# Twelve channel blocks of a hybrid gMLP and attention step by seven block products over the token halves, with the latent projection ahead of them

## The chip, the cores and the metric

The kernel runs on one core of a Trainium2 chip. The metric is the device time of one execution in microseconds (us), as the median of several runs.

Engines are called as the profile calls them: PE (matrix products and transposes), DVE, ACT and POOL (elementwise work), SP (issues most of the DMAs here).

## What is computed

1152 tokens (1024 samples, 128 prompt) of width 1024 go through one projection `w_in`, whose columns feed two head groups; both end in one output projection.

```python
h = _rmsnorm(x, norm_g) * (1 + scale) + shift
u, v, g_a, c_q, c_kv, k_rope, g_b = _split_in(h @ w_in)
a_out = _chunk_mlp(u, v, w_s, b_s, g_v) * jax.nn.silu(g_a)      # gelu(u) * mixed, gated
q = (_rmsnorm(c_q, q_norm_g) @ w_uq).reshape(B, L, MLA_HEADS, QK_NOPE + QK_ROPE)
ckv = _rmsnorm(c_kv, kv_norm_g)
...
y = jnp.concatenate([a_out, attn * jax.nn.silu(g_b)], axis=-1) @ w_o
return x + gate * y
```

`u`, `g_a` and `g_b` have 512 channels each: 12 blocks of 128, numbered 0 to 11 in the kernel (0 to 3 are `u`, 4 to 7 `g_a`, 8 to 11 `g_b`). `v` has 512 columns; `c_q`, `c_kv` and `k_rope` together have 448 (here: the latents, `z`). All is in float32, which the kernel feeds to PE as a high and a low half (type fp32r): each product is three matmuls, high by high, high by low, low by high.

## The kernel before

Tokens are cut into nine tiles of 128 (tile 8 is the prompt), and the 1024 inputs into NK = 8 chunks `k`. The modulated input `h` stands transposed in three tiles `area0` to `area2`, each of 384 tokens, high and low for every `k`. By the time of the profiled execution the stages are:

- 0 to 58 us, prologue: x and the adaLN weights `ada` arrive by DMA, PE makes the modulation (L331, strips of 32 rows by 256) and the transposes, ACT and DVE split `h`, PE begins the `v` projection (L360 to L362) of tiles 0 to 4.
- 58 to 139 us: a list scheduler (`class Plan`) orders steps that were given an engine, a cost, needs, a priority and counted resources. In it stand `v` of the other tiles, the position mixing, and the first channel blocks (L632, 384 columns).
- 139 to 253 us: blocks 3 to 11 by the loop `for i in range(3, 12)`, each for three groups of 384 tokens (`channels`, `passes3`, L151 to L153). The weights of a block come as one load `w2r` (512 KB) and are split into `w2h` (POOL, L108) and `w2l` (DVE, L105, through `lo_of`). ACT applies GELU or SiLU, POOL multiplies the result into `mixA` (L693, L640 in the planned part). Beside it the adaLN gate sums are made on DVE: `matvec` multiplies and adds eight 256-wide rows (L310, L312) for two conditions, four times; PE sums them over the partitions (`gate_row`, L716). The latent weights `w_q` are loaded and split here too (L108, L301 on POOL).
- 253 to 318 us: the latents `z` of nine tiles (`z_chunk`, L940 to L942, 448 columns), with their statistics, the transposes of `c_q`, the query weights (`fold`) and most queries (`q_nope`, `q_rope`) beside them, in an order made by `merged` and `later`.
- 318 to about 332 us, transition: keys and the last queries; then scores, softmax and attention until 535 us, and the output projection until the end. Both are ordered by lists of steps.

The order within each engine is the program's order (the four compute engines are scheduled by hand); SP issues the DMAs in program order.

Of the kernel before, what the change touches and what calls it, by code (L numbers as in the profile page):

```python
# [18 lines left out]
P = 128  # L19
NT = 9  # L20
# [8 lines left out]
W1 = 8  # L29
W2 = 0  # L30
# [10 lines left out]
class Plan:  # L41
# [8 lines left out]
    def run(self):  # L50
# [3 lines left out]
        while left:  # L54
# [4 lines left out]
            for s in left:  # L59
                _, _, key, eng, cost, fn, deps, takes, gives, lag = s  # L60
                if self.free[eng] > now + 1e-6 or any(self.made.get(d, 1e9) > now + 1e-6 for d in deps):
                    continue
                if any(self.resources[r] < 1 for r in takes):
                    continue
                for r in takes:
                    self.resources[r] -= 1
                fn()
                self.free[eng] = now + cost
                self.made[key] = now + cost + lag
                back += [(now + cost + lag, r) for r in gives]  # L70
                left.remove(s)
                self.log.append((now, cost, eng, key))
                moved = True
                break
            if not moved:
                later = [t for t in (*self.free.values(), *self.made.values(), *(b[0] for b in back)) if t > now + 1e-6]
                assert later, [s[2] for s in left]
# [10 lines left out]
def tile_hymba_step(ctx: ExitStack, tc: tile.TileContext, I, O):  # L88
# [177 lines left out]
    def slot(i, name, shape, dt=F32):  # L266
        return (va if i < 8 else vb).tile([P] + shape, dt, tag=f"S{i}", name=name)
# [3 lines left out]
    area = [ht.tile([P, 16, GW], F32R, tag=f"area{g}", name=f"area{g}") for g in range(3)]  # L271
    hh = {(k, g): area[g][:, 2 * k, :] for k in range(NK) for g in range(3)}
    hl = {(k, g): area[g][:, 2 * k + 1, :] for k in range(NK) for g in range(3)}
# [4 lines left out]
    def load_wv(k):  # L278
        wvr[k] = w1.tile([P, 512], F32, tag="wr", name=f"wvr{k}", bufs=2)
        nc.sync.dma_start(wvr[k], I["w_v"][k])  # L280

    def load_x(t, i):
        xt[t] = slot(i, f"x{t}", [1024])
# [30 lines left out]
    def load_ada(k, slots):  # L314
        out = []
        for hf_ in range(2):
            ch = slot(slots[hf_], f"ada{k}{hf_}", [4, 256])
            nc.sync.dma_start(ch, I["ada_ss"][k][:, hf_ * 4 : hf_ * 4 + 4, :])
            out += [ch[:, i, :] for i in range(4)]
        return out  # L320
# [12 lines left out]
    def mod_copy(k):  # L333
        rowsb[k] = va.tile([P, 256], F32, tag="acc", name=f"rows{k}", bufs=2)
# [14 lines left out]
    def modulate(k, g, c0, c1, ps, cond):  # L349
        w = c1 - c0  # L350
        hf = va.tile([P, GW], F32, tag="hf", name=f"hf{k}{g}{c0}", bufs=3)
        S.activation(hh[k, g][:, c0:c1], ps, AF.Identity, bias=at[:, k, cond, 0:1], scale=at[:, k, cond, 1:2])
        S.activation(hf[:, :w], ps, AF.Identity, bias=at[:, k, cond, 0:1], scale=at[:, k, cond, 1:2])
        lo_of(hl[k, g][:, c0:c1], hf[:, :w], hh[k, g][:, c0:c1])

    def v_terms(k, t, acc):
        g, j = t // 3, t % 3
        sl = slice(j * P, (j + 1) * P)
        a, b = hh[k, g][:, sl], hl[k, g][:, sl]
# [6 lines left out]
    ADA = ((0, 1), (2, 3), (4, 5))  # L366

    def load_k(k):
        if k < NK:
            ada[k] = load_ada(k, ADA[k % 3])  # L370
            load_wv(k)

    wsT = vb.tile([P, 4, P], F32, tag="wsT", name="wsT")
    bsb = vb.tile([P, 4, P], F32, tag="bsb", name="bsb")
    kvg = mc.tile([P, P], F32, tag="kvg", name="kvg")

    w2raw, w2hi, w2lo = {}, {}, {}

    def load_w2(i):
        w2raw[i] = slot(4 + i % 2, f"w2r{i}", [8, P])  # L380
        nc.sync.dma_start(w2raw[i], I["w_t"][i])

    def split_w2(i):
        a, b = ((0, 1), (2, 3), (6, 7))[i % 3]
        w2hi[i] = slot(a, f"w2h{i}", [8, P], F32R)
        w2lo[i] = slot(b, f"w2l{i}", [8, P], F32R)
        pool_copy(w2hi[i], w2raw[i])
        lo_of(w2lo[i], w2raw[i], w2hi[i])
# [27 lines left out]
    def h_pe(k, g):  # L416
        xps[k, g] = pst.tile([P, 512], F32, tag="t", name=f"xT{k}{g}")
        transposes(k, [3 * g, 3 * g + 1, 3 * g + 2], xps[k, g])

    def h_ev(k, g):  # L420
        modulate(k, g, 0, GW, xps[k, g][:, :GW], 0)
# [6 lines left out]
    with tc.manual_schedule(engines=engines):  # L428
# [13 lines left out]
        for t in (0, 1, 2):  # L442
            load_x(t, 6 + t)
        load_k(0)
        for t in (3, 4, 5):
            load_x(t, 6 + t)
# [9 lines left out]
        h_pe(0, 0)  # L456
        ssq1 = vb.tile([P, 3], F32, tag="ssq", name="ssq3", bufs=2)
        square(V, 3, ssq1[:, 0:1])
        h_ev(0, 0)
# [8 lines left out]
        h_pe(0, 1)  # L468
        h_ev(0, 1)
        modulation(1)  # L470
        for k in range(1, NK):
# [23 lines left out]
            if k == 4:  # L495
                load_w2(0)
                load_w2(1)
                nc.sync.dma_start(wsT, I["wsT"])
                nc.sync.dma_start(bsb, I["b_s"].broadcast_to([P, 512]))
                nc.sync.dma_start(kvg, I["kv_g"].broadcast_to([P, P]))  # L500
# [10 lines left out]
    gv, ssv = {}, {}  # L511
    plan = Plan()
    step = plan.add

# [3 lines left out]
    def rsqrt_steps(key, pool, ssq, n, width, tag, prio, deps, before=None):  # L518
        cell = {}

        def begin():
            if before is not None:
                before()
# [5 lines left out]
        step(f"{key}.-1", "V", 0.08, begin, deps, prio)  # L529
        for i in range(count):  # L530
            step(f"{key}.{i}" if i < count - 1 else key, "V", 0.08, lambda i=i: cell["ops"][i](), [f"{key}.{i - 1}"], prio, lag=0.13)
        return cell

    def split_steps(i, deps):
        def hi():
            a, b = ((0, 1), (2, 3), (6, 7))[i % 3]
            w2hi[i] = slot(a, f"w2h{i}", [8, P], F32R)
            w2lo[i] = slot(b, f"w2l{i}", [8, P], F32R)
            pool_copy(w2hi[i], w2raw[i])

        step(f"w2h{i}", "G", 1.01, hi, [f"w2r{i}", *deps], 2)
# [1027 lines left out]
```

## Time and profile before

| | |
|---|---|
| runs | 632.67, 633.30 and 637.25 us, median 633.3 us |
| profiled execution, first to last instruction | 634.2 us, mean granted PE clock 0.987 |
| PE, DVE, ACT, POOL busy | 615.5, 366.3, 257.8 and 182.6 us |
| DMA | 46.3 MB, mean 73 GB/s over the span |

A row of the groups of instructions reads: line, engine, operation, output<-inputs by the program's names, shape and number; then busy time in us and mean ns of one; then the idle time of the engine before them and what ended it. A row of a timeline begins with its start and its duration in us; what stands in brackets is the engine's idle time before it and the instruction that ended it. Durations of pipelined PE instructions overlap, so PE's price is read from the distance of starts or from the chain that ended last. A row of stretches gives for each engine the busy us and the number of instructions, then PE's granted clock, the share of the DMA engines and GB/s.

### The profile page before, as it was taken

The numbers are of one execution on the slowest core, as the hardware profiler recorded it, in microseconds if no ns is written. First come the engines' busy times: TensorE is split into PE (matmuls) and PEld (weight loads), VectorE is DVE, ScalarE is ACT, GpSimd is POOL, SyncE is SP. The second block draws the span as 40 slices with busy tenths as digits, with TensorE's granted clock in tenths as the row PEclk, the third lists the DMA queues.
The fourth block names the chain that finished last, engine by engine and source line by source line (L and its number), as shares of the span: only waits on it lengthen the run. The fifth ranks groups of instructions, "written<-read, shape, count | busy, mean of one in ns | idle before, by whom it ended". The sixth has DMA issues, their size and how long they took to land.

```text
span 634.2 us, 9897 instructions
## 1 busy us (share of the span) xinstructions
PE 615.5 (97%) x3715; PEld 557.2 (88%) x3715; DVE 366.3 (58%) x922; ACT 257.8 (41%) x613; POOL 182.6 (29%) x219
## 2 busy tenths in 40 slices
PE   7799999999999999999989999999999999999995
PEld 6577889999999999999978899999999988888884
DVE  4437447237866200567886665776766755387655
ACT  4355784012111111455456555555555543132212
POOL 2534202344436510233353221332222341000001
PEclk9799999999999999999989999999999999999998
DMA  8976100015023330000010000001000112523311
GB/s 318 321 247 215 66 1 2 1 38 209 18 99 114 125 119 0 26 13 2 0 41 1 1 1 1 1 1 35 34 1 33 34 68 75 192 99 133 105 62 66
DMA packets 17119, 46.32 MB, mean 73 GB/s; under 512 B 1952, under 2 KB 6448, under 8 KB 17072
## 3 DMA queue, kind: packets, MB, share of 16 engines
q1 hardware_dynamic: 16928, 45.51, 20.6%
q8 instruction: 29, 0.48, 0.3%
q10 hardware_dynamic: 144, 0.20, 0.1%
q14 instruction: 18, 0.15, 0.1%
HBM read 40.87 MB, written 4.83 MB: 72 GB/s over the span
## 4 chain that ended last, share of the span: by engine, by line
PE 90%; DVE 3%; DMA 2%; ACT 2%; issue 1%; SPq 1%; POOL 0%; ACTq 0%
PE tp L152 6%; PE tp L632 6%; PE tp L153 6%; PE tp L151 6%; PE pT L1095 5%; PE w L1342 5%; PE w L1343 5%; PE w L1344 5%; PE o L1121 3%; PE o L1119 3%; PE s L1048 3%; PE s L1049 3%; PE o L1120 3%; PE s L1051 3%; PE s L1052 3%; PE s L1050 3%
## 5 line engine op out<-in xcount | busy, mean ns | idle before, releaser
L105 DVE TENSOR_TENSOR pl<-pT,ph 128x512 fp32r<-128x512 f32 x81 | 55.5, 687 | 47.7 <-ACT ph L1099 47.5
L1039 POOL TENSOR_SCALAR e<-e,rs 128x1280 f32<-128x1280 f32 x32 | 42.8, 1337 | 132.3 <-DVE rs L1038 118.0
L153 PE MATMUL tp<-area,w2l 128*128 128x384 f32 x216 | 72.7, 336 | 0.0
L152 PE MATMUL tp<-area,w2h 128*128 128x384 f32 x216 | 72.6, 336 | 0.0
L151 PE MATMUL tp<-area,w2h 128*128 128x384 f32 x216 | 72.6, 336 | 0.0
L1033 ACT ACTIVATE e<-s,nb,scl 128x256 f32<-128x256 f32 x64 | 56.1, 881 | 36.9 <-DVE nb L1027 36.8
L1099 ACT CAST ph<-pT 128x512 fp32r<-128x512 f32 x80 | 45.4, 589 | 42.7 <-PE pT L1095 40.0
L1095 PE MATMUL pT<-ident,e 128*128 128x128 f32 x320 | 47.9, 273 | 0.7 <-DVE pl L105 0.7
L1119 PE MATMUL o<-ph,vh 128*128 128x256 f32 x160 | 47.4, 296 | 0.0
L1121 PE MATMUL o<-ph,vl 128*128 128x256 f32 x160 | 44.7, 280 | 0.0
L105 DVE TENSOR_TENSOR w2l<-w2r,w2h 128x1024 fp32r<-128x1024 f32 x12 | 20.3, 1688 | 42.1 <-POOL w2h L108 42.1
L1120 PE MATMUL o<-pl,vh 128*128 128x256 f32 x160 | 44.6, 279 | 0.0
L1344 PE MATMUL w<-area,ml 128*128 128x512 f32 (+1 forms) x114 | 43.2, 379 | 0.0
L1095 PEld LDWEIGHTS pT<-ident,e 128*128 128x128 f32 x320 | 37.5, 140 | 4.4 <-DVE pl L105 1.5
L151 PEld LDWEIGHTS tp<-area,w2h 128*128 128x128 f32 x216 | 40.7, 188 | 0.6
L152 PEld LDWEIGHTS tp<-area,w2h 128*128 128x128 f32 x216 | 40.7, 188 | 0.2
L153 PEld LDWEIGHTS tp<-area,w2l 128*128 128x128 f32 x216 | 40.7, 188 | 0.0
L1023 DVE TENSOR_REDUCE m<-s 128x1 f32<-128x1024 f32 x32 | 38.9, 1216 | 1.5 <-PE s L1052 1.5
L1048 PE MATMUL s<-kch,area 128*128 128x512 f32 (+2 forms) x100 | 39.1, 391 | 0.0
L632 PE MATMUL tp<-area,w2h 128*128 128x384 f32 x144 | 37.1, 339 | 0.0
L1049 PE MATMUL s<-kcl,area 128*128 128x512 f32 (+2 forms) x100 | 35.5, 355 | 0.0
L1051 PE MATMUL s<-krh,area 128*128 128x512 f32 (+2 forms) x100 | 35.3, 353 | 0.0
(295 smaller groups left out, 1599.7 us busy)
## 6 DMA issues: line engine op xcount, KB each, us to landing
ada<-in_ada_ss SPq DMA_DIRECT2D x16, 512.0 KB, 9.6
w2r<-in_w_t SPq DMA_DIRECT2D x12, 512.0 KB, 3.6
xr<-in_x SPq DMA_DIRECT2D x9, 512.0 KB, 4.6
adag<-in_ada_g SPq DMA_DIRECT2D x8, 512.0 KB
wor<-in_w_o SPq DMA_DIRECT2D x8, 512.0 KB, 3.3
out_y<-y SPq DMA_DIRECT2D x8, 512.0 KB, 3.7
x<-in_x SPq DMA_DIRECT2D x6, 512.0 KB, 9.1
wvr<-in_w_v SPq DMA_DIRECT2D x8, 256.0 KB, 8.4
```

The source lines that it names most:

```text
L105: V.tensor_tensor(lo, src, f32(hi), op=ALU.subtract)
L151: T.matmul(ps, wh, xh, start=j == 0, stop=False)
L152: T.matmul(ps, wh, xl, start=False, stop=False)
L153: T.matmul(ps, wl, xh, start=False, stop=j == n - 1)
L632: T.matmul(tps[i, g][:, :GW], w_[i][:, k, :], x_[k, g], start=k == 0 and j == 0, stop=k == NK - 1 and j == 2)
L1033: S.activation(e[:, sl], src, AF.Exp, bias=nb, scale=scl[:, t : t + 1], accum_out=su[:, i : i + 1])
L1048: T.matmul(ps, qh_, kch[:, sl], start=True, stop=False)
L1095: T.transpose(ps[:, w : w + P], es[t, h][:, c * P : (c + 1) * P], ident)
L1119: T.matmul(o, vh[:, kt, :], ph[:, sl], start=c == 0, stop=False)
L1120: T.matmul(o, vh[:, kt, :], pl[:, sl], start=False, stop=False)
L1121: T.matmul(o, vl[:, kt, :], ph[:, sl], start=False, stop=c == n - 1)
L1344: T.matmul(ps, b, woh[k][:, c0:c1], start=False, stop=k == NK - 1)
```

## The change

**Token projection.** The 1024 sample tokens are cut into two halves `x`, the 1024 inputs into two halves `y`, and `h` lies in four tiles `areas[x, y]` of 512 tokens by 512 inputs; the prompt lies in `areap`. The 12 channel blocks are taken in six pairs `j`. For each pair the 2 x 2 block product (token halves by input halves by the two blocks of the pair) is made from seven products `ph` (in the order 1, 2, 5, 6, 7, 4, 3) instead of eight, in the manner of Strassen and Winograd: four of the products have as moving operand a sum or difference of blocks of `h` (steps `s1x` to `s4y`, L937 to L951, then split anew into high and low), and as weights sums or differences of weight blocks (`ws`, L786 to L798); the results are added up on DVE and POOL (L886 to L902). A product is 4 chunks of three matmuls of 512 columns (L828). The prompt tile goes by matmuls of its own (L977: 256 columns, then a transpose, L996). These replace all the matmuls of L151 to L153 and L632 of the channel blocks.

**Order.** `z` (L697 to L699) is now a step of the planner beside `v` and is done before the products; its raw results are kept in `zraw`, the statistics are made once for all tiles. The rope keys, the query weights and queries are planner steps beside and behind the last products. The planner may choose DVE or POOL for a step (`VG`), or ACT or POOL (`SG`). Its own costs do not count the one engine's work against the other's.

**Gate sums.** `gate_steps` replaces `gate_sums` and `gate_row`: the same strips as in the modulation, 32 matmuls of 32 x 256 on PE (L728), and four additions per `j` on DVE (L736). Its load tile `adag` has one buffer (it had two).

**Loads.** `w2r` (two), `wsT`, `bsb` and `kvg` are no longer issued ahead of the last `ada` load. Weights of the channel blocks come in halves of 256 KB (`wr`, four at a time). In the attention, four pieces of `w_o` are loaded early and four late (five and three before), and 16 instead of 20 terms of the output projection stand early.

```diff
-    area = [ht.tile([P, 16, GW], F32R, tag=f"area{g}", name=f"area{g}") for g in range(3)]
+    areas = {(x, y): ht.tile([P, 4, 2, 512], F32R, tag=f"area{x}{y}", name=f"area{x}{y}") for x in range(2) for y in range(2)}
+    areap = ht.tile([P, 8, 2, P], F32R, tag="areap", name="areap")
...
-                load_w2(0)
-                load_w2(1)
-                nc.sync.dma_start(wsT, I["wsT"])
...
+    VG, COST = "VG", (0.75, 1.3)
+    SG, HIGH = "SG", (0.62, 0.75)
+    def rounded(e, out, in_):
+        S.copy(out, in_) if e is S else pool_copy(out, in_)
...
-    for i in range(3, 12):
...
-        gs = gate_sums(i - 4) if 4 <= i < 8 else None
-        for g in range(3):
-            channels(i, g)
...
+    def gate_steps(j):
...
+                T.matmul(cell["ps"][32 * s_ : 32 * s_ + 32, 0:256], csp[:, 4 * i + s_, :], cell[i][:, s_, :], start=i == 0, stop=i == 1)
...
+    A11, A12, A21, A22 = areas[0, 0], areas[0, 1], areas[1, 0], areas[1, 1]
+    SEQ = [(ph, j) for ph in (1, 2, 5, 6) for j in range(NJ)] + [(7, j) for j in (2, 3, 4, 5, 0, 1)]
+    SEQ += [(ph, j) for js in ((0, 1), (2, 3, 4, 5)) for ph in (4, 3) for j in js]
+    MOVING = {1: A11, 2: A12, 5: A21, 6: A11, 7: A21, 4: A22, 3: A11}
...
+    NEEDS = {1: ((0, 0),), 2: ((1, 0),), 5: ((0, 0), (0, 1)), 6: ((1, 1),), 7: ((1, 1), (0, 1)), 4: ((1, 0),), 3: ((1, 1),)}
+    def weight_steps(ph, j, prio):
...
+                    e.tensor_tensor(tsum[j], r(0), tsum[j], op=ALU.subtract)
...
+        step(f"wh{ph}{j}", SG, HIGH, high, loaded + before, prio, takes=("wop", "slot", "slot"))
+        step(f"w{ph}{j}", "V", 0.75, low, [f"wh{ph}{j}"], prio, gives=gives)
...
+    def product_steps(ph, j, prio, deps):
...
+            for i, (a, b) in enumerate(((0, 0), (0, 1), (1, 0))):
+                first, last = k == 0 and i == 0, k == 3 and i == 2
+                T.matmul(ps, w[a][:, k, :], x[:, k, b, :], start=first and ph in FIRST, stop=last, skip_group_check=ph not in FIRST)
...
+    def sum_steps():
...
+            step(f"s1x.{k}", VG, COST, lambda e, q=q, st=st: e.tensor_tensor(st("a"), q(A21, 0), q(A21, 1), op=ALU.add), ["openB"], 3.0 + 0.01 * k, takes=("st", "slot"))
+            step(f"s1y.{k}", VG, COST, lambda e, q=q, s_new=s_new: e.tensor_tensor(s_new(), q(A22, 0), q(A22, 1), op=ALU.add), ["openB"], 3.0 + 0.01 * k)
...
+            step(f"s2x.{k}", VG, COST, lambda e, k=k, q=q: e.tensor_tensor(ss[k], ss[k], q(A11, 0), op=ALU.subtract), [f"a5.{k}"], 3.2 + 0.01 * k)
...
+        plan.resources.update(psa=1, pst=2, slot=6, gv=3, ga=1, raw=4, wop=3, tmp=2, praw=2, pw=2, st=3, r2=1)
```

**How the instructions move.** Three places are shown, for DVE and POOL in the stage of the channel blocks, and for DVE behind it.

On DVE, before, at the channel blocks 5 and 6 (`accg` are the gate sums, `w2l` the low half of a block's weights):

```order
L105 TENSOR_TENSOR w2l_1433<-w2r_1402,w2h_1432 128x1024
L310 TENSOR_SCALAR accg_1494<-adag_1495,csp 128x256 x2
L312 SCALAR_TENSOR_TENSOR accg_1494<-adag_1495,csp,accg_1494 128x256 x6
L312 SCALAR_TENSOR_TENSOR accg_1494<-adag_1505,csp,accg_1494 128x256 x8
L105 TENSOR_TENSOR log_1517<-accg_1494,hig_1515 128x512
L105 TENSOR_TENSOR w2l_1548<-w2r_1492,w2h_1547 128x1024
```

and now, among the products of `ph` 1 and 2 (`pw` are low halves of the prompt's weights, `wop` of a product's weights, `ss` and `sta` the sums of token blocks, `area` their low halves):

```order
L968 TENSOR_TENSOR pw_1606<-praw_1563,pw_1605 128x512
L968 TENSOR_TENSOR pw_1616<-praw_1578,pw_1615 128x512
L937 TENSOR_TENSOR ss_1608<-ss_1608,sta_1591 128x512
L114 TENSOR_TENSOR area_114<-ss_1567,area_114 128x512
L114 TENSOR_TENSOR wop_1642<-wr_1132,wop_1641 128x512
L937 TENSOR_TENSOR ss_1650<-ss_1650,sta_1624 128x512
L114 TENSOR_TENSOR wop_1664<-wr_1140,wop_1663 128x512
L968 TENSOR_TENSOR pw_1674<-praw_1632,pw_1673 128x512
```

The gate sums are gone, and in their place stand 512-wide instructions with two inputs from SBUF, which the products wait for.

On POOL, before, at the same place:

```order
L301 TENSOR_TENSOR ql_1610<-wqr_1607,qh_1609 128x448
L693 TENSOR_TENSOR mixA<-mixA,tmp_1461 128x384
L108 TENSOR_SCALAR w2h_1547<-w2r_1492 128x1024
L693 TENSOR_TENSOR mixA<-mixA,tmp_1489 128x384
L693 TENSOR_TENSOR mixA<-mixA,tmp_1544 128x384
```

and now:

```order
L941 TENSOR_TENSOR ss_1608<-area_115 128x512
L940 TENSOR_TENSOR sta_1624<-area_114 128x512
L117 TENSOR_SCALAR wop_1641<-wr_1132 128x512
L941 TENSOR_TENSOR ss_1650<-area_115 128x512
L117 TENSOR_SCALAR wop_1663<-wr_1140 128x512
L944 TENSOR_TENSOR ss_1567<-ss_1567,area_112 128x512
L945 TENSOR_TENSOR ss_1567<-ss_1567,area_112 128x512
L947 TENSOR_TENSOR stb_1711<-area_115 128x512
```

POOL now makes sums that products wait for, where it mostly multiplied results into `mixA`.

On DVE behind the last product's result (`mixB<-mixB,pr`), now (`qn` and `qr` are queries, `qrT` transposed rope queries, `kT` transposed keys):

```order
L902 TENSOR_TENSOR mixB<-mixB,pr_2976 128x512
L114 TENSOR_TENSOR area_113<-qn_3018,area_113 128x512
L1195 TENSOR_TENSOR r_3053<-qr_3027,rope_2769 128x512
L114 TENSOR_TENSOR area_114<-qn_3041,area_114 128x512
L114 TENSOR_TENSOR area_113<-qn_3055,area_113 128x512
L1195 TENSOR_TENSOR r_3094<-qr_3065,rope_2769 128x512
L1246 TENSOR_TENSOR area_115<-qrT_3080,area_115 64x4x128 x2
L114 TENSOR_TENSOR area_113<-qn_3086,area_113 128x512
L1246 TENSOR_TENSOR area_115<-qrT_3101,area_115 64x4x128 x2
```

Before, this kind of work stood between the statistics of the latents, one tile at a time:

```order
L883 TENSOR_TENSOR qr_2621<-qr_2600,rope 128x256
L123 TENSOR_TENSOR zt<-zr 128x2
L124 TENSOR_TENSOR zt<-zt,zw 128x2
L125 SCALAR_TENSOR_TENSOR zr<-zt,zr 128x2
L123 TENSOR_TENSOR zt<-zr 128x2
```

All of it has moved from beside the 65 us of `z` to behind the products, except what the planner found room for beside the last of them.

More of the change, by code (lines that the diff above doesn't have):

```diff
@@ L59, in run @@
             for s in left:
-                _, _, key, eng, cost, fn, deps, takes, gives, lag = s
-                if self.free[eng] > now + 1e-6 or any(self.made.get(d, 1e9) > now + 1e-6 for d in deps):
+                _, _, key, engs, cost, fn, deps, takes, gives, lag = s
+                free = [n for n, e in enumerate(engs) if self.free[e] <= now + 1e-6]
+                if not free or any(self.made.get(d, 1e9) > now + 1e-6 for d in deps):
                     continue
-                if any(self.resources[r] < 1 for r in takes):
+                if any(self.resources[r] < takes.count(r) for r in takes):
                     continue
@@ L836, in cq_transpose @@
-    def cq_transpose(t):
-        ps = pst.tile([P, 512], F32, tag="t", name=f"cqT{t}")
-        for q in range(2):
-            T.transpose(ps[:, q * P : (q + 1) * P], zt[t][:, q * P : (q + 1) * P], ident)
-        src = ps[:, 0:256].rearrange("p (q c) -> p q c", q=2)
-        dh = cqh[:, :, t * P : (t + 1) * P]
-        def low():
-            lo_of(cql[:, :, t * P : (t + 1) * P], src, dh)
-            made.add(("cq", t))
-        later(0.4, lambda: S.copy(dh, src))
-        later(0.85, low)
```

1128 lines of the change are left out of this document (709 added, 419 removed).

## The prediction

> **What bounds the kernel now.** I read the page's first part and the chain that ended last, then the stretches by stage.
>
> ```profile
> PE 615.5 (97%) x3715; PEld 557.2 (88%) x3715; DVE 366.3 (58%) x922; ACT 257.8 (41%) x613; POOL 182.6 (29%) x219
> ...
> PE 90%; DVE 3%; DMA 2%; ACT 2%; issue 1%; SPq 1%; POOL 0%; ACTq 0%
> ```
>
> ```profile
> 58.00:139.00 81.00, 81.00 (x467) 74.45 (x460) 33.91 (x106) 37.60 (x128) 24.38 (x23) 1.00 0.07 23
> 139.00:253.00 114.00, 114.00 (x656) 112.87 (x656) 51.08 (x84) 16.68 (x32) 46.02 (x40) 1.00 0.28 96
> 253.00:318.00 65.00, 64.98 (x376) 60.87 (x375) 44.96 (x182) 32.50 (x90) 22.44 (x63) 1.00 0.04 10
> 318.00:347.00 29.00, 26.43 (x152) 23.16 (x151) 21.89 (x55) 16.81 (x45) 14.03 (x20) 0.94 0.07 22
> ```
>
> From 58 to 318 us PE is the bound, full at full clock. DVE has 51.1 of 114 us in the channel blocks, POOL 46.0. So PE time taken out of this stretch is saved one for one, as long as the other engines keep up. That is the question, since the change pays for fewer products with elementwise work.
>
> **PE's part.** Prices come from the chain (start, duration, number of matmuls) and from distances of starts:
>
> ```profile
> 45.34 1.04 PE mod L331 x16
> ```
>
> ```profile
> 114.01 24.96 PE tp L632 x144
> ```
>
> ```profile
> 168.10 0.46 PE gps L716 x2
> ```
>
> ```profile
> 63.77 0.39 PE L360 MATMUL vacc<-vh,area 128*128 128x512 f32 x1
> ...
> 64.45 0.39 PE L360 MATMUL vacc<-vh,area 128*128 128x512 f32 x1
> ```
>
> ```profile
> 323.45 0.28 PE L151 MATMUL qr<-wrh,cqh 128*128 128x256 f32 x1
> 323.57 0.28 PE L152 MATMUL qr<-wrl,cqh 128*128 128x256 f32 x1
> ```
>
> A 384-column matmul takes 24.96/144 = 0.173 us, a 512-column one 0.68/3 = 0.227 (three between the two starts), a 256-column one 0.12. Removed: 864 x 0.173 = 149.8 us. Added: 7 products x 6 pairs x 4 chunks x 3 = 504 x 0.227 = 114.4; the prompt's 144 x 0.12 = 17.3; 12 transposes, at most 0.12 each, 1.4. Gate sums: four strips at 1.04 in place of four rows at 0.46, 2.3 more. Sum: **-14.4 us**. The matmuls of v, z, keys and queries do the same work as before.
>
> **The shared port of DVE and POOL.** These rows are from the channel blocks: POOL first, then DVE.
>
> ```profile
> 138.87 1.02 POOL L640 TENSOR_TENSOR mixA<-mixA,tmp 128x384 f32<-128x384 f32 x1
> 139.86 2.03 POOL L108 TENSOR_SCALAR w2h<-w2r 128x1024 fp32r<-128x1024 f32 x1
> ...
> 194.05 1.05 POOL L108 TENSOR_SCALAR w2h<-w2r 128x1024 fp32r<-128x1024 f32 x1
> ...
> 199.31 4.80 POOL L693 TENSOR_TENSOR mixA<-mixA,tmp 128x384 f32<-128x384 f32 x1 [3.23 <-ACT tmp L690]
> ```
>
> ```profile
> 138.94 2.03 DVE L105 TENSOR_TENSOR w2l<-w2r,w2h 128x1024 fp32r<-128x1024 f32 x1 [4.57 <-POOL w2h L108]
> ...
> 156.71 0.69 DVE L105 TENSOR_TENSOR log<-accg,hig 128x512 fp32r<-128x512 f32 x1 [0.69 <-ACT hig L708]
> ...
> 168.43 1.22 DVE L105 TENSOR_TENSOR w2l<-w2r,w2h 128x1024 fp32r<-128x1024 f32 x1
> ...
> 197.61 5.62 DVE L312 SCALAR_TENSOR_TENSOR accg<-adag,csp,accg 128x256 f32<-128x256 f32 x14
> ```
>
> The same DVE split takes 1.22 us where POOL is quiet and 2.03 where POOL had begun 0.07 earlier; the same POOL copy takes 1.05 and, begun inside that split, 2.03. A POOL multiply of some 1.02 us took 4.80 while DVE ran accumulations back to back. So a DVE instruction with two SBUF inputs and a POOL instruction do not run at once: the second waits. From 138.94 to 140.97 the split lasts 0.81 longer than its 1.22, so it ran from 139.75 on, and the multiply ended at 139.89: the two overlap by some 0.14 us at the hand-over. DVE instructions that read PSUM do not show it:
>
> ```profile
> L105 DVE TENSOR_TENSOR pl<-pT,ph 128x512 fp32r<-128x512 f32 x81 | 55.5, 687 | 47.7 <-ACT ph L1099 47.5
> ```
>
> This mean, 687 ns, is the undisturbed one, though POOL multiplies beside it. The Trainium skill ("SBUF — State Buffer", section "Who interferes with whom") states it as an exclusive lock on a port pair that a DVE instruction with two SBUF inputs and a GpSimd instruction share, held by the first for its whole instruction; by this rule, which speaks against the change, the hand-over would save nothing. The trace agrees that the second waits, and shows the 0.14 us of overlap.
>
> Now the products need both engines. I count the program's order from the first sum of token blocks up to the low weights of product 4 of pair 2, where the lag is largest: 101 DVE instructions of 128x512 with two SBUF inputs (token sums, their low halves, low weights of the products and the prompt), 52 POOL additions or multiplies of 128x512, 18 POOL copies of 128x512. On PE 402 matmuls of 512, the prompt's 144 of 256 and 18 small ones lie ahead of it: 402 x 0.227 + 17.3 + 2.3 = 110.9 us. Prices for POOL:
>
> ```profile
> 192.92 1.16 POOL L301 TENSOR_TENSOR ql<-wqr,qh 128x448 fp32r<-128x448 f32 x1
> ```
>
> ```profile
> L568 POOL TENSOR_TENSOR gv<-gv,vv1r 128x512 f32<-128x512 f32 x1 | 1.0, 1039 | 1.2 <-DVE vv1r L125 1.2
> ...
> L108 POOL TENSOR_SCALAR vh<-wvr 128x512 fp32r<-128x512 f32 x1 | 0.6, 619 | 0.0
> ```
>
> An addition of two full operands at 512 columns is an estimate of 1.16 x 512/448 = 1.3 us; the row of 1.04 has one narrow operand and is the lower bound. At full length the port has 101 x 0.69 + 52 x 1.3 + 18 x 0.62 = 69.7 + 67.6 + 11.2 = 148.5 us of work, 37.6 more than PE. If each of the 171 instructions saves a hand-over of 0.13, it is 126.3, **15.4 more than PE**; with 1.04 for the addition 112.8, 1.9 more. Since the sums cannot start before the last z has read the area that their buffers take (the step that opens them waits for all z), some 3 us ahead of the first product, and only three products' weights fit ahead of PE, there is no lead that could absorb it. After that point the port has less to do than PE, so the lag is not made worse, nor given back. I take 15 us, because additions of two full operands are what is issued and DVE and POOL alternate for most of the stage; the ends are 2 and 38. DVE alone (134 instructions of 512 at 0.69 and some small ones, 106 us of PE's 137) and POOL alone (57 x 1.3 + 18 x 0.62 = 85) would fit, ACT with some 71 us too.
>
> **Transition.** Before, PE stood 29.00 - 26.43 = 2.6 us between 318 and 347, with a clock of 0.94 (0.06 x 29 = 1.7 us). The queries now stand behind the products: 24.7 us of PE work by the same prices, and for DVE behind the last result 17 instructions of 128x512, 16 of 64x512 and 8 small ones.
>
> ```profile
> L910 DVE TENSOR_TENSOR area<-qrT,area 64x512 fp32r<-64x512 f32 x12 | 8.3, 689 | 6.9 <-ACT area L909 6.7
> ```
>
> 33 x 0.69 + 8 x 0.3 = 25 us, as long as PE's part, and in the order PE, ACT, DVE, PE for every tile; the first scores wait for the keys' low halves, 28 instructions down that queue (25 x 0.69 + 3 x 0.3 = 18.2 us). Two such waits stand there today:
>
> ```profile
> 321.18 0.39 PE L151 MATMUL qr<-wrh,cqh 128*128 128x256 f32 x1 [0.47 <-ACT cqh L847]
> ...
> 323.23 0.39 PE L153 MATMUL qr<-wrh,cql 128*128 128x256 f32 x1 [1.55 <-DVE cql L105]
> ```
>
> I take 3 us more idle than before; nothing if every wait finds other matmuls, 8 if PE waits for DVE all along and the lower clock that the 0.94 shows comes a second time.
>
> **Loads.** The single gate buffer lets a load start only when the four matmuls of the half before are done:
>
> ```profile
> w2r<-in_w_t SPq DMA_DIRECT2D x12, 512.0 KB, 3.6
> ```
>
> ```profile
> 46.82 0.42 SPq L498
> ```
>
> 3.6 us to landing with an issue of 0.42 on SP, against gate halves that stand 3.8 to 5.1 us of PE work apart: +1 us (0 to 3). Behind the waiting strip on PE stand z matmuls, which wait too. The move of z itself I cost at nothing: its 216 matmuls take the same PE time, and the eight splits of `w_q` (at most 0.62 on POOL and 0.69 on DVE each, by the rows above for 512 columns) lie beside v, where DVE has 33.9 and POOL 24.4 of 81 us; without that cover the first z tile would wait for some 1.3 us per chunk, 10 us in all. The last `ada` load is issued some 2 us earlier, past five other loads; the wait that this can end is
>
> ```profile
> L331 PE MATMUL mod<-ada,csp 128*32 128x256 f32 x8 | 0.6, 391 | 0.3 <-DMA ada<-in_ada_ss 0.3
> ```
>
> 0.3 us. The weights of the products and the prompt now come in 78 halves of 256 KB, 20.4 MB in some 145 us, 140 GB/s, under half of what the prologue's first slices reach:
>
> ```profile
> GB/s 318 321 247 215 66 1 2 1 38 209 18 99 114 125 119 0 26 13 2 0 41 1 1 1 1 1 1 35 34 1 33 34 68 75 192 99 133 105 62 66
> ```
>
> I cost them at nothing, hidden behind the products of 2.7 us each that stand one or two ahead; if that cover is gone, a product waits for a landing of up to 3.6 us. The fourth late piece of `w_o` and the four early terms moved to the end: 0 to +1, I take 0.5.
>
> **Sum.** Profiled execution 634.2 - 14.4 + 15 + 3 + 1 - 0.3 + 0.5 = 639.0; the runs' median lies 0.9 below that execution's span, so **638 us**, 0.7% over 633.3. Own range: lag 8 to 24 us, that is 631 to 647. A measurement of this kernel can tell a change of about 1% (627 to 639.6 us) from none.
>
> **Rivals.**
>
> *The port is hidden.* If DVE's and POOL's instructions interleave so that POOL's half is mostly waiting for loads and results anyway, the lag is 0 to 2 and only PE counts: 638 - 15 = 623 (620 to 627). For it: each engine alone fits, the additions may cost 1.04, the prompt's matmuls need no sums and can be put in front. Against it: the 4.80 us multiply, and 2.03 for 1.05, in a stage with half this work.
>
> *The lock at full length.* If hand-overs save nothing, since DVE runs its instructions in bursts and POOL, whose sums DVE needs next, is starved as at 199.31, the lag at that product is 24 (additions at 1.04) to 38 us: 638 - 15 + 24 to 38 = 647 to 661, say 655, slower. It decides from a port load of 125 us on, where PE's 110.9 and the other terms' gain of 14 are used up. That is what the skill's rule of the lock gives.
>
> *The transition becomes the bound.* The products stay as forecast, but PE waits for DVE's 25 us with the half clock on top: +8, 646, slower. For it: the waits of 1.55 and 0.47 us; against it: keys' transposes and queries of other tiles lie between.
>
> **Chances.** Forecast 0.50 (of it 0.03 faster, 0.28 within 1%, 0.19 slower), hidden port 0.25 (0.24 faster), full lock 0.15, transition 0.10 (nearly all slower). So faster 0.27, same 0.30, slower 0.43. The range of 621 to 656 takes in the hidden port but for its lowest end, and the full lock up to its middle.
>
> **What would show it.** Right: PE idle by 10 us or more between the first and the last product, ended by DVE's `wop` and `area` low halves or by sums; DVE's 128x512 with two SBUF inputs at a mean of over 0.9 us instead of 0.69, POOL's additions over 1.6, while instructions from PSUM stay near 0.69; PE's busy time down by some 14 us; PE idle of 5 to 6 us at the transition. Wrong: PE over 98% busy in the products (hidden port), or idle of over 25 us there (full lock), or the idle time ended by DMA (`wr`), for which I count nothing.

## The result, and the profile after

The changed kernel takes 662.6 us in the median (661.75 to 663.19) against 634.3 us, a ratio of 1.043 (95% interval 1.039 to 1.046): slower by 4.3%. The forecast was 638 us, within 1%, with a range of 621 to 656; the measured time lies 6.6 us above the range. One run of a later experiment (high halves on ACT) took 770 us at a granted clock of 0.75 and is left out of its median.

The page of the changed kernel, engines and chain:

```profile
span 660.4 us, 9804 instructions
...
PE 618.8 (94%) x3567; PEld 524.7 (79%) x3567; DVE 437.3 (66%) x874; ACT 301.6 (46%) x672; POOL 225.4 (34%) x203
...
PE 75%; DVE 11%; issue 4%; DMA 4%; ACT 2%; POOL 2%; SPq 0%; ACTq 0%; POOLq 0%; DVEq 0%
```

PE no longer carries the chain alone: 25% of it are other engines and issue. DVE is busy for 71 us more than before, POOL for 43.

The stretches of the changed kernel, cut at the first product, the last product, the first score and the last value matmul:

```profile
0.00:58.00 58.00, 50.71 (x337) 36.90 (x339) 26.25 (x78) 28.71 (x56) 20.46 (x24) 0.91 0.73 264
58.00:153.50 95.50, 92.51 (x524) 77.08 (x517) 44.77 (x141) 46.40 (x159) 19.55 (x21) 1.00 0.29 95
153.50:320.20 166.70, 149.30 (x705) 122.07 (x704) 145.59 (x176) 69.75 (x128) 108.72 (x81) 0.96 0.38 122
320.20:353.20 33.00, 27.82 (x177) 23.43 (x175) 22.17 (x37) 21.62 (x43) 17.51 (x23) 0.98 0.08 25
353.20:563.60 210.40, 209.31 (x1417) 190.59 (x1418) 140.45 (x285) 112.39 (x236) 56.16 (x53) 0.99 0.06 21
563.60:660.40 96.80, 89.10 (x420) 74.59 (x418) 58.03 (x159) 22.71 (x53) 2.99 (x3) 0.98 0.31 109
```

and of the kernel before, from its first score on:

```profile
329.90:540.40 210.50, 209.42 (x1433) 190.34 (x1431) 139.80 (x285) 113.41 (x239) 60.03 (x57) 1.00 0.08 27
540.40:634.20 93.80, 86.35 (x408) 72.32 (x406) 58.46 (x159) 22.11 (x52) 2.98 (x3) 0.98 0.30 106
```

The first score starts at 353.2 instead of 329.9: 23.3 of the 26.2 us lie ahead of it. Attention takes the same time (210.4 and 210.5 us), and 3.0 us lie at the end, where 12 matmuls (408 to 420) have come over from the attention: 12 x 0.227 = 2.7. The product stage, 166.7 us, is the place: DVE is busy for 145.6 of them, PE stands for 17.4 and has a clock of 0.96. What ended PE's waits there:

```profile
PE pps L977 <- DVE pw L968: 13.1, 6, 3.3
PE pr L828 <- ACT wop L543: 2.3, 2, 2.1
PE pr L828 <- DVE wop L114: 1.3, 3, 0.6
PE pr L828 <- DVE s L897: 0.6, 1, 0.6
```

DVE's low halves of the prompt's weights (`pw`) lead the list. DVE's groups in the stage, with two SBUF inputs and then with one input from PSUM, and two of POOL:

```profile
L114 DVE TENSOR_TENSOR wop<-wr,wop 128x512 fp32r<-128x512 f32 x21 | 20.6, 983 | 4.3 <-ACT wop L543 4.3
L114 DVE TENSOR_TENSOR wop<-tsum,wop 128x512 fp32r<-128x512 f32 x18 | 20.5, 1150 | 1.0 <-POOL wop L117 1.0
L968 DVE TENSOR_TENSOR pw<-praw,pw 128x512 fp32r<-128x512 f32 x19 | 18.9, 1010 | 1.4 <-ACT pw L543 0.8 <-POOL pw L117 0.5
L114 DVE TENSOR_TENSOR area<-ss,area 128x512 fp32r<-128x512 f32 x12 | 14.3, 1222 | 0.0
...
L902 DVE TENSOR_TENSOR uu<-uu,pr 128x512 f32<-128x512 f32 x4 | 2.7, 680 | 2.0 <-PE pr L828 2.0
```

```profile
L968 POOL TENSOR_TENSOR pw<-praw,pw 128x512 fp32r<-128x512 f32 x5 | 7.5, 1503 | 6.6 <-ACT pw L543 6.6
...
L947 POOL TENSOR_TENSOR stb<-area 128x512 f32<-128x512 f32 x4 | 6.4, 1606 | 0.0
```

The same shape takes 0.98 to 1.22 us with both inputs in SBUF and 0.68 with one in PSUM; POOL's additions take 1.5 to 1.6. So two of the marks that the prediction named for the shared port are there: DVE at over 0.9 us, and about 0.69 from PSUM. POOL's additions, 1.58 in the mean over the stage, stay just under the 1.6 that it named. PE stands for longer than the 10 us named, but for the prompt's `pw` rather than for `wop`, `area` or sums. And PE's busy time has not fallen by 14 us: it is 618.8 against 615.5. In the product stage alone it is 149.3 us at a clock of 0.96, against 138.9 at 1.00 in experiment 2 for the same matmuls.

### The profile page after: what moved, and what is told of

It is laid out like the page before. It is cut to its first block, busy times and chain, and to the rows that moved or that the text cites. A ratio compares the mean times of both kernels' runs of the same rounds, so it can differ in the third digit from the quotient of the medians.

```text
span 660.4 us, 9804 instructions
## 1 busy us (share of the span) xinstructions
PE 618.8 (94%) x3567; PEld 524.7 (79%) x3567; DVE 437.3 (66%) x874; ACT 301.6 (46%) x672; POOL 225.4 (34%) x203
## 2 busy tenths in 40 slices
DMA packets 29840, 60.48 MB, mean 92 GB/s; under 512 B 3024, under 2 KB 13664, under 8 KB 29792
## 4 chain that ended last, share of the span: by engine, by line
PE 75%; DVE 11%; issue 4%; DMA 4%; ACT 2%; POOL 2%; SPq 0%; ACTq 0%; POOLq 0%; DVEq 0%
PE pr L828 11%; PE pT L1504 5%; PE w L1754 5%; PE w L1753 5%; PE w L1755 5%; PE s L1461 3%; PE o L1528 3%; PE o L1530 3%; PE s L1465 3%; PE s L1462 3%; PE s L1463 3%; PE o L1529 3%; PE s L1464 3%; PE vacc L390 3%; PE pps L977 2%
## 5 line engine op out<-in xcount | busy, mean ns | idle before, releaser
L828 PE MATMUL pr<-area,wop 128*128 128x512 f32 x504 | 128.4, 403 | 4.3 <-ACT wop L543 2.3
L828 PEld LDWEIGHTS pr<-area,wop 128*128 128x128 f32 x504 | 93.8, 193 | 25.5 <-ACT wop L543 3.6
L1753 PE MATMUL w<-area,areap 128*128 128x512 f32 (+1 forms) x152 | 57.8, 381 | 0.0
L1755 PE MATMUL w<-area,ml 128*128 128x512 f32 (+1 forms) x152 | 57.5, 378 | 0.0
L1754 PE MATMUL w<-area,areap 128*128 128x512 f32 (+1 forms) x152 | 57.5, 378 | 0.0
L1461 PE MATMUL s<-kch,area 128*128 128x512 f32 (+1 forms) x96 | 38.8, 404 | 0.8 <-DVE areap L114 0.8
L977 PE MATMUL pps<-pw,areap 128*128 128x256 f32 x144 | 25.9, 312 | 13.1 <-DVE pw L968 13.1
L977 PEld LDWEIGHTS pps<-pw,areap 128*128 128x128 f32 x144 | 23.6, 210 | 17.1 <-DVE pw L968 14.5
L1844 POOL TENSOR_TENSOR z<-y,fg 128x256 f32<-128x256 f32 (+1 forms) x3 | 3.0, 998 | 95.4 <-DVE y L1839 95.4
L1463 PE MATMUL s<-kch,area 128*128 128x512 f32 (+1 forms) x96 | 34.7, 361 | 0.0
L1462 PE MATMUL s<-kcl,area 128*128 128x512 f32 (+1 forms) x96 | 34.7, 361 | 0.0
L1465 PE MATMUL s<-krl,area 128*128 128x512 f32 (+1 forms) x96 | 34.7, 361 | 0.0
```

The source lines that it names most:

```text
L828: T.matmul(ps, w[a][:, k, :], x[:, k, b, :], start=first and ph in FIRST, stop=last, skip_group_check=ph not in FIRST)
L977: T.matmul(out, areap[:, 2 * y + k, b, :], pw[y][a][:, :, k, :], start=y == 0 and k == 0 and i == 0, stop=y == 3 and k == 1 and i == 2)
L1461: T.matmul(ps, qh_, kch[:, sl], start=True, stop=False)
L1753: T.matmul(ps, a, woh[k][:, c0:c1], start=k == 0, stop=False)
L1754: T.matmul(ps, a, wol[k][:, c0:c1], start=False, stop=False)
L1755: T.matmul(ps, b, woh[k][:, c0:c1], start=False, stop=k == NK - 1)
```

## The experiments

The theories: the **port** (DVE's instructions with two SBUF inputs and POOL's that read SBUF exclude each other, and this is where the time goes), against the **order** (PE is held by what it meets too early in its own row, or an engine by its own work, and the long DVE instructions are off the path).

**1. The cost by itself.** A kernel that only runs DVE and POOL instructions of 128x512 (multiplies, in the place of additions); "two" has two inputs from SBUF, "bank" one from PSUM, "set" is a memset.

```diff
+        phase("a", ["two"], [], 24, 0)
+        phase("b", [], ["two"], 0, 16)
+        phase("c", [], ["one"], 0, 16)
+        phase("e", ["two"], ["two"], 48, 24)
+        phase("f", ["two"], ["one"], 48, 48)
+        phase("g", ["bank"], ["two"], 48, 24)
+        phase("h", ["two", "bank"], ["two"], 48, 24)
+        phase("i", ["two"], ["set"], 48, 48)
+        phase("j", ["one"], ["two"], 48, 24)
```

> This kernel computes nothing of the reference (its outputs are zeros). It only runs DVE and POOL instructions of 128x512 in stretches: DVE alone, POOL alone, and both side by side, free of each other. Lock theory (a DVE instruction with two SBUF inputs and any POOL instruction that reads SBUF exclude each other): 48 DVE additions beside 24 POOL ones take about 48 x 0.69 + 24 x 1.3 = 64 us if the lock is held at full length, about 55 if each of the 72 hand-overs saves 0.13 us; one engine or the other may run in bursts. With one input from PSUM the same DVE instructions take 0.69 beside POOL and the stretch is 33 us. POOL memsets, which read nothing, do not slow DVE. Rival (slower memory for both, not a lock): both slow down by a common factor, with one PSUM input too.

Its groups; the second letter of an output's name is the stretch:

```profile
L128 DVE TENSOR_TENSOR de<-oe,ec 128x512 f32<-128x512 f32 x48 | 54.5, 1213 | 0.0
L140 POOL TENSOR_SCALAR pf<-of 128x512 f32<-128x512 f32 x48 | 48.7, 1046 | 15.8 <-DVE of L121 15.8
L128 DVE TENSOR_TENSOR df<-of,ee 128x512 f32<-128x512 f32 x48 | 48.4, 1084 | 0.0
L132 DVE TENSOR_SCALAR dj<-oj 128x512 f32<-128x512 f32 x48 | 41.7, 949 | 0.0
L138 POOL TENSOR_TENSOR ph<-oh,eg 128x512 f32<-128x512 f32 x24 | 40.2, 1709 | 1.3 <-DVE oh L121 1.3
L138 POOL TENSOR_TENSOR pe<-oe,ec 128x512 f32<-128x512 f32 x24 | 40.0, 1703 | 1.3 <-DVE oe L121 1.3
L138 POOL TENSOR_TENSOR pj<-oj,ei 128x512 f32<-128x512 f32 x24 | 33.6, 1436 | 9.0 <-DVE oj L121 9.0
L138 POOL TENSOR_TENSOR pg<-og,ef 128x512 f32<-128x512 f32 x24 | 29.5, 1288 | 1.3 <-DVE og L121 1.3
L128 DVE TENSOR_TENSOR di<-oi,eh 128x512 f32<-128x512 f32 x48 | 29.0, 695 | 0.0
L130 DVE TENSOR_TENSOR dg<-og,bank 128x512 f32<-128x512 f32 x48 | 28.8, 680 | 0.0
L128 DVE TENSOR_TENSOR dh<-oh,eg 128x512 f32<-128x512 f32 x24 | 27.2, 1133 | 0.0
L142 POOL MEMSET pi<- 128x512 f32 x48 | 22.7, 525 | 0.0
L138 POOL TENSOR_TENSOR pb<-ob,ea 128x512 f32<-128x512 f32 x16 | 19.6, 1262 | 19.0 <-DVE ob L121 19.0
L130 DVE TENSOR_TENSOR dh<-oh,bank 128x512 f32<-128x512 f32 x24 | 16.2, 675 | 0.0
L128 DVE TENSOR_TENSOR da<-oa,first 128x512 f32<-128x512 f32 x24 | 14.5, 691 | 0.0
```

Alone, DVE makes one such instruction in 14.5/24 = 0.605 us and POOL one in 19.6/16 = 1.225. Side by side (e) 24 pairs take POOL's 40.0 us, 1.67 a pair against 1.83 for the two in turn; DVE's other 24 then run at its own pace, 54.5 us in all. That is the lower of the two numbers expected, though by other terms: the expectation took the durations 0.69 and 1.3 and saved 0.13 at every hand-over, where the paces of 0.605 and 1.225 leave 0.16 to be saved per pair. The two take turns, one by one; neither runs in bursts. With one input from PSUM (g) neither loses anything, and against memsets (i) DVE doesn't. In stretch h an instruction with one input from PSUM stands between every two with two from SBUF, and a round still takes 1.67 us (40.2 for 24): it finds room in POOL's turn. So it is a lock, and not a slower memory.

**2. POOL writes and does not read.** The changed kernel in its own order on DVE, ACT and PE; POOL's planned work beside the products is replaced, an addition by two memsets of the same output and a copy by one. It leaves out what POOL computes there.

```diff
-                    fn(self.engines[eng])
+                    fn(self.engines[eng] if eng != "G" or key[:2] in ("qr", "kr") else self.writer)
...
+    class Writer:
+        def tensor_tensor(self, out, a, b, op=None):
+            o = out if out.dtype == F32 else f32(out)
+            for _ in range(2):
+                G.memset(o, 1.0)
...
+        if e is plan.writer:
+            G.memset(f32(out), 1.0)
+            return
```

> The changed kernel in its own order on every engine, but each POOL addition or multiply of the planner's beside the products is replaced by two POOL memsets of the same output (2 x 0.525 us instead of 1.26), and each POOL copy by one: POOL does not read SBUF there, the outputs are wrong, DVE, ACT and PE do what they did. Lock theory: DVE's 128x512 with two SBUF inputs go back to 0.69 us, DVE's busy time in the product stage from 146 to some 106 us, the stage from 167 to 143 to 150, 639 to 646 us in all. Rival (the order and the waits within the queues, or loads): the stage stays over 160, 655 or more.

631.9 us against 635.8 (0.993, 0.991 to 0.995), 31 us less than the changed kernel. Its product stage, and two of DVE's groups in it:

```profile
154.80:293.70 138.90, 138.90 (x705) 117.66 (x704) 96.40 (x175) 70.36 (x128) 69.44 (x135) 1.00 0.46 146
```

```profile
L114 DVE TENSOR_TENSOR wop<-wr,wop 128x512 fp32r<-128x512 f32 x21 | 14.7, 703 | 5.5 <-ACT wop L555 5.5
...
L114 DVE TENSOR_TENSOR area<-ss,area 128x512 fp32r<-128x512 f32 x12 | 8.0, 687 | 1.0 <-ACT area L555 0.9
```

PE never stands, its clock is 1.00, and the stage takes 138.9 us instead of 166.7. DVE's busy time for the same instructions falls from 145.6 to 96.4: some 49 us were waits for the port. The total is even less than the port theory's number, and it rules out the order: DVE, ACT and PE run the same instructions in the same order in both traces, and the loads are the same 60.48 MB. What the run doesn't separate is that POOL is also shorter here (69 for 109 us) and doesn't wait for its inputs. That can shorten DVE's waits before an instruction, but the 49 us are in the instructions' own durations.

**3. No POOL at all beside the products.** Every result is computed, only in other places; the first line lets a step with a single engine keep its pair of costs (in e2 and in experiment 6 too).

```diff
-                if len(engs) > 1:
+                if isinstance(cost, tuple):
...
-    VG, COST = "VG", (0.75, 1.3)
+    VG, COST = ("V",), (0.75, 1.3)
...
-    SG, HIGH = "SG", (0.62, 0.75)
+    SG, HIGH = ("S",), (0.62, 0.75)
```

> The changed kernel with every addition and multiply of the planner's on DVE and every high half on ACT; POOL has next to nothing left beside the products. Lock theory: DVE's 128x512 go back to 0.69 us, DVE has some 167 x 0.69 + 38 x 0.65 + 5 = 145 us of work beside 139 of PE, the stage takes 145 to 152 instead of 167, 641 to 648 us in all, though DVE has half as much again to do. Rival (each engine is limited by its own work and order): DVE was at 146 of 168 us already, so 57 more instructions make the stage longer or leave it, 662 to 690.

649.0 us (1.022, 1.019 to 1.026). The stage and the transition:

```profile
151.90:299.60 147.70, 142.04 (x702) 116.45 (x702) 123.84 (x219) 79.10 (x146) 1.12 (x2) 1.00 0.43 137
299.60:339.50 39.90, 30.32 (x178) 24.56 (x177) 35.69 (x69) 23.12 (x46) 6.32 (x10) 0.88 0.03 8
```

With 57 more additions and multiplies on DVE, DVE is busy for 22 us less (its additions are back at 0.69 us), and the stage is 19 us shorter, inside the expected 145 to 152, at a clock of 1.00. The rival's sign was wrong. The total is 1 us over what I expected, since the transition grew by 7 us; experiment 6 looks for the reason.

**4. Copies off the port, prompt later.** Two single steps: all high halves on ACT, and the prompt's pairs 2 to 5 later in PE's row.

```diff
...
-    SG, HIGH = "SG", (0.62, 0.75)
+    SG, HIGH = ("S",), (0.62, 0.75)
```

> The changed kernel with all high halves rounded on ACT instead of ACT or POOL: 18 POOL copies leave the product stage (18 x 0.62 = 11 us of port time), ACT gets 18 x 0.59 more. Lock theory: the product stage (167 us now) gets 8 to 11 us shorter, 652 to 655 us in all. Rival (PE is held by the prompt's weights, which it meets too early in its own order, and the longer DVE and POOL instructions are off the path): within 3 us of 662.

```diff
-PROMPTP = (7.2, 7.8, 8.6, 9.2, 9.8, 10.4)
-PROMPTL = (1.605, 1.625, 1.645, 1.665, 1.685, 1.705)
+PROMPTP = (7.2, 7.8, 12.4, 13.0, 13.6, 14.2)
+PROMPTL = (1.605, 1.625, 1.765, 1.785, 1.805, 1.825)
```

> The changed kernel with the prompt's matmuls and weights for pairs 2 to 5 later in PE's order (beside products 5 and 6 instead of 1 and 2). 13.1 of the 17.4 us for which PE stands in the product stage are waits for the prompt's low weights. Rival (the prompt's place in PE's row): these waits go, 648 to 652 us. Lock theory: a prompt piece costs the port about as much (0.69 and a share of the copies) as it gives PE (0.71), so the waits go over to the products' weights and sums: 657 to 665.

High halves on ACT: 663.5 us (1.043, 1.038 to 1.049), no gain. That misses my 652 to 655 and is the number of the rival (within 3 us of 662).

```profile
153.00:323.10 170.10, 149.31 (x705) 122.21 (x704) 140.13 (x173) 79.23 (x146) 98.12 (x66) 0.96 0.37 119
```

DVE's busy time fell by 5 us (145.6 to 140.1), POOL's by 11, and the stage still took 170.1. The planner, with other costs, made another order, in which DVE stood 30 instead of 21 us for others, so this run alone can't tell the two theories apart; experiment 2, where the order is kept, does. What this lock costs can't be worked out by counting the port's time alone.

Prompt later: 662.5 us (1.044, 1.040 to 1.047), as the port theory said, and not the rival's 648 to 652. PE's waits in the product stage of that run:

```profile
PE pr L828 <- DVE wop L114: 9.0, 7, 3.1
PE pps L977 <- DVE pw L968: 8.6, 4, 3.2
PE pps L977 <- POOL pw L968: 2.5, 3, 1.7
```

The products' weights now hold PE for 9.0 us (1.3 before). The prompt's still do so for 8.6 by DVE and 2.5 by POOL, so only a part of the waits went over; but PE stands no less in all, 21.7 us (168.9 - 147.2) for 17.4. Most of what PE waits for is what DVE owes next; the prompt was the first creditor.

**5. No token sums.** The sums of token blocks and their splits are left out, the products take unsummed blocks.

```diff
-        sum_steps()
+        for k in range(4):
+            for ph in (5, 6, 7, 3):
+                plan.made[f"a{ph}.{k}"] = 0.0
...
```

> The changed kernel (DVE and POOL shared as there) with the sums of token blocks and their splits left out: the products take unsummed blocks, so the outputs are wrong. PE has the same matmuls. 36 additions, 16 low and 16 high halves go. Lock theory: DVE's work with POOL's holds falls by some 52 x 0.6 + 20 x 1.1 = 50 us to under 100, and the product stage goes to PE's 139 to 143 us, 635 to 640 in all. Rival (the products' own weight sums, splits and the order keep PE waiting): the stage stays over 155, 650 us.

640.2 us (1.006, 1.004 to 1.009). Its product stage:

```profile
152.20:298.00 145.80, 141.99 (x704) 118.55 (x703) 105.69 (x150) 60.65 (x111) 70.03 (x58) 0.99 0.44 139
```

DVE's load is 40 us lower and PE stands 3.8 us. DVE and POOL still share the port here, but DVE is no longer the late engine. The stage is just over the 143 us expected, the total at the upper end of the 635 to 640, and both are far from the rival's 155 and 650. The run takes work off ACT and POOL too, so it doesn't show DVE's share by itself.

**6. Attempts on the rest.** From the kernel without POOL: POOL allowed behind the products by the planner (e5), the gate weights in pieces of 256 KB with two buffers on top of that (e7), the latents' statistics early on top of both (e8); and the statistics in the middle (e10) or the rope steps issued on POOL in the unchanged order (e11).

```diff
# e5: and the same for the steps y, kra, krb, kr; z
-            step(f"{key}x", VG, half, lambda e: cross(e, 0), [f"{key}c", "rt"], 1.5, takes=("r2", "slot"))
+            step(f"{key}x", "VG", half, lambda e: cross(e, 0), [f"{key}c", "rt"], 1.5, takes=("r2", "slot"))
# e7
-            cell[i] = vc.tile([P, 4, 256], F32, tag="ada", name=f"adag{j}{i}")
+            cell[i] = vc.tile([P, 2, 256], F32, tag="ada", name=f"adag{j}{i}", bufs=2)
# e8 (2.4) and e10 (3.0): likewise for the chain of the statistics
-            step(f"kvn{t}", "V", 0.36, lambda t=t: kv(t), ["zr"], 6 + 0.1 * t)
+            step(f"kvn{t}", "V", 0.36, lambda t=t: kv(t), ["zr"], 2.4)
# e11
-                    fn(self.engines[eng])
+                    fn(self.engines["G" if key[:2] in ("qr", "kr") else eng])
```

> The kernel without POOL beside the products, but with POOL allowed again for the rope keys and rope queries behind them. Without POOL anywhere the stretch from the last product to the first score took 39.9 us instead of 33.0, since DVE had that work too. Lock theory with DVE as the late engine: the product stage stays at 148 us and the transition falls back to 33 to 36, 642 to 645 us in all. Rival (POOL at the transition slows DVE by the same lock, so nothing comes back): 649.

> The kernel without POOL in its own order, but each step of the rope keys and rope queries is issued on POOL where that order had it on DVE; nothing else is moved. Without POOL the product stage took 147.7 us and the transition 39.9; where POOL was allowed again by the planner, 156.0 and 32.5, at another order of DVE. Lock theory with DVE as the late engine: the stage keeps 148 to 151, the transition falls to 33 to 36, 642 to 646 us. Rival (what the stage lost came from POOL's rope work in it, not from the order): the stage is back at 154 to 158 and the sum is 649 again.

> As the run with POOL behind the products alone, and the gate weights come in pieces of 256 KB with two buffers instead of 512 KB with one. If the single buffer costs the 3.0 us of idle PE in the stage of v and z: 2 to 3 us less than that run. If the wait is for the loads' rate: no difference (within 1).

> As the run with gate quarters, and the latents' statistics and the scaling of the key latents (9 small DVE instructions and a chain of 13) stand early in the product stage instead of at its end. If the keys' wait at the transition (5.6 us without POOL) is their place in DVE's order: 3 to 5 us less than gate quarters. If the product stage's early part is what DVE is latest in, it gives back the same there: no difference.

> The kernel without POOL, and the latents' statistics and key scaling in the middle of the product stage instead of at its end. If the 5.6 us wait of the keys at the transition is their place in DVE's order and DVE has room in the middle: 643 to 646 us. If DVE is late all through the products: 649 or more, the wait having moved.

| run | us | ratio to before, interval | product stage | to first score |
|---|---|---|---|---|
| e3 no POOL | 649.0 | 1.022, 1.019 to 1.026 | 147.7 | 39.9 |
| e5 POOL behind, by the planner | 649.3 | 1.022, 1.018 to 1.026 | 156.0 | 32.5 |
| e11 rope on POOL, order kept | 648.7 | 1.022, 1.018 to 1.025 | 149.4 | 39.9 |
| e10 statistics in the middle | 652.6 | 1.026, 1.024 to 1.029 | 157.4 | 34.0 |
| e7 gate quarters | 657.5 | 1.034, 1.029 to 1.039 | 154.7 | 34.5 |
| e8 statistics early | 662.9 | 1.044, 1.039 to 1.049 | 162.5 | 34.4 |

None beats the kernel before. e5 ended at its rival's 649, but not for its reason: the transition did come back (32.5), and the stage lost 8 us. In e11 the stage stayed short with POOL's rope work in it, so these 8 us came from DVE's other order, as the first of its expectations had it; but the transition did not fall, so it isn't DVE's rope work that fills those 39.9 us. PE's longest wait there is the same as without POOL (the keys behind the scaled latents, 6.0 and 5.6 us). Moved forward (e10) that wait went, the transition fell to 34.0, and the stage paid 10 us for it. Still earlier, and on top of the gate pieces (e8), the transition stayed where e7 has it and the stage paid 8 us more: neither of its expectations. In these versions what is put earlier for the end is owed in the middle, though DVE is busy for only 123 to 129 us of the stage; why it is late there is argued from its order and not shown. The gate pieces did shorten the wait for their loads (3.4 to 1.1 us), but the stage of v and z got longer by 1.5 us, and the whole by 8 in the median, where 2 to 3 less were expected (the stretches in the table are of a run of 653.4 us); why is not settled.

## Why the prediction was wrong, step by step

**PE's part, -14.4 us: nearly right.** With nothing to wait for, the stage takes PE 138.9 us (e9), where the prediction counted 137, so the part is some -12.5. e9 ends 0.7% ahead of the kernel before; the rest goes to the transition, the loads and the end. PE's busy time falls by 10.4 us in e9 (615.5 to 605.1): of the 4 that are missing, 1.9 are these, and some 3 are in the transition, where PE is busy for 27.8 us and 24.7 were counted.

**The shared port: the mechanism right, the size wrong; this is the step that failed.** The term was "I take 15 us" of lag, with 8 to 24 in the forecast's own range; the runs show 27.8 (166.7 against 138.9). The price of the lock was not the fault. By the isolated run a pair of additions costs 1.67 us, a DVE addition with a POOL copy 48.4/48 = 1.01; put into the prediction's count (52 pairs, 18 with copies, 31 DVE instructions at 0.605) they give 86.7 + 18.2 + 18.8 = 123.7 us, 12.8 more than PE. The fault was to set the port's work alone against PE's, as though the port were busy all the time and everything else beside it. DVE takes its instructions in order. Its own 96.4 us (e9), among them the additions from PSUM, which don't wait for the port but stand in the same queue, and the 49.2 us for which it stood at the port make 145.6, already more than PE's 138.9; with 21.1 us in which it waited for ACT, POOL, PE and loads it is the 166.7. I had the 106 us of DVE and the port's work in two separate sums and said of the first that it would fit.

This divides the measured stage; it does not forecast it. That DVE's queue sets the stage's time is borne out by the runs in which that queue is shorter: with DVE busy for 123.8, 105.7 and 96.4 us (e3, e6, e9) the stage takes 147.7, 145.8 and 138.9. But DVE's other work need not add to the port's: in stretch h it found room in POOL's turn. How much of it did so in the kernel's order, and so how the 27.8 us split into lock and queue, stays open.

**The clock.** I costed lower clock only at the transition. In the changed kernel's product stage 0.96 over 166.7 us is 6.7 us. It belongs to the 27.8: where PE doesn't stand (e9) it is 1.00. With the 17.4 us of standing that makes 24.1; the other 3.7 I can't assign.

**The transition: +3 forecast.** The way from the last product to the first score takes 33.0 us with 24.7 of PE work counted, 8.3 over; before, the idle time and the lower clock came to some 4. So +4, inside the 0 to 8. e9 leaves it at 32.9, so it doesn't come from the products' lag.

**Loads: +1 forecast.** PE stands 3.0 us in the stage of v and z, 1.5 of them for `adag` and 1.4 for the chain of a statistic, which I had not named; together that is the end of my range of 0 to 3.

**The end: +0.5 forecast, +3.0 measured.** The four terms that left the attention are 12 matmuls of 0.227 us; I had given them and a load 0 to 1 together, though the price stood in the same text. The attention, which gave them up, should have become shorter by as much; it did not (210.4 against 210.5 us, the clock 0.99 against 1.00), and e9, at a clock of 1.00, still takes 209.3.

**Together** the measured terms are -12.5 + 27.8 + 4 + 3 + 3 = 25.3 of the 26.2 us by which the profiled execution is longer.

**The rivals.** The full lock had the right size by luck, for a reason that the isolated run refutes: hand-overs do overlap, and DVE and POOL take turns. Its lag of 24 to 38 holds the measured 27.8; the sum, 647 to 661, misses by 2 us for the end and the loads. The Trainium skill's rule ("SBUF — State Buffer", section "Who interferes with whom") is right here in who contends: two SBUF inputs do, an input from PSUM doesn't (0.680 us beside POOL), and a POOL instruction that only writes doesn't (0.695). By the same page of the Trainium skill (section "SBUF: two separate sides") the lock is held for the whole instruction; the isolated run shows 0.16 us less per pair. The hidden port was wrong: POOL is busy for 109 of 167 us, its waits at the port included, and DVE stood at the port for 49. The transition as the bound was wrong too: it costs +4, with the products' lag in place.

## What to carry to other kernels

Before work is given to POOL because DVE is full, see whether DVE's instructions have both inputs in SBUF: then the two take turns almost like one engine, POOL's share is the dearer one (1.225 against 0.605 us for the same instruction), and leaving POOL idle can be faster (here by 13.6 us). Sum the late engine's whole queue, its own work and what it stands for at the port and for others, and compare that with the bound; a resource's own load says only that it can't be less. And a schedule whose planner prices each engine by itself is no evidence that they can run together: a single look at one replaced instruction (memsets in the place of additions) shows what sharing costs (here 27.8 us of the stage).

## What the runs showed of the hardware

- DVE and POOL alternate strictly when both have work for the port: 1.67 us a pair of 128x512 instructions with two SBUF inputs. The 4.80 us multiply of the kernel before, that I read as starvation, stood against 256-wide accumulations; in the changed kernel's product stage none of POOL's 128x512 additions takes over 1.83 us.
- A DVE instruction with one input from PSUM does not wait, and fits into POOL's turn: a round of both DVE kinds and one of POOL's takes the same 1.67 us (stretch h).
- A DVE instruction with only one SBUF input can wait too. In stretch j of the isolated run a multiply by a constant in fp32 took 0.949 us in the mean over 48, about half of them beside POOL's two-input instructions, which took 1.44 instead of 1.26; the 23 that were left after POOL's last took 7.8 us together. The copies of the same size between the stretches took 0.43. Why a single input contends here and a PSUM one doesn't, these runs don't show.
- POOL's memset of 128x512 costs DVE's two-input instructions nothing: 0.695 us, as alone (0.691). The memset takes 0.525 us there; no run has it alone.
